# Block differences on GpSimd instead of VectorE, and a longer run of idle products at the start

## The chip, the cores and the metric

One core of a Trainium2 chip runs the kernel. Its engines work side by side, each through its own queue in order: TensorE (PE, with the weight loads shown apart as PEld), VectorE (DVE), ScalarE (ACT), GpSimd (POOL), and SyncE (SP), which issues most of the DMAs. The metric is device time in microseconds, the median of several executions. One more execution was taken with the hardware profiler, and every row shown below is from it.

## The reference

An encoder block for 1024 positions of width 1024, with 16 learned meta tokens ahead of them. Everything is float32.

```python
u = _rms_norm(h, pre_w)
z = u @ w_in                                  # one projection, split into q, k, v, gates
rq, rk, rv, rg, aq, ak, av, ag, gr, ga = _split_in(z)
...
o_r = _bidirectional_retention(rq, rk, rv, lg_f, lg_b)[:, META_PAD:]
...                                           # group norm per head
o_r = o_r * ret_nw * jax.nn.silu(rg)
y_r = o_r @ w_rb
...
o_a = _windowed_sink_attention(aq, ak, av, sink)
o_a = o_a * jax.nn.silu(ag)
y_a = o_a @ w_ab
mix = jax.nn.sigmoid(gr) * y_r + jax.nn.sigmoid(ga) * y_a
out = mix @ w_o
return h + _rms_norm(out, post_w)
```

## The kernel before

**Products in two halves.** A float32 matrix is kept as a high part of type `fp32r` and the rest, the low part. `mm3` (lines 74 to 79) forms a product from three matmuls: high by high on line 76, low by high on line 77, high by low on line 78. So whatever becomes an operand is split first: ScalarE or GpSimd copies the high part (`nc.scalar.copy`, or `pool_hi` on line 89), and VectorE takes the source minus the high part (`dve_lo`, line 92, two inputs in SBUF).

**The beginning.** While the first inputs are still on their way, TensorE runs products of a zeroed tile, `idle` (lines 310 to 313). Then come eight steps `qk0_mm(k)`, each over 128 rows of the width. For each step ScalarE makes the high part of x (line 333, tile `big`) and VectorE the low part (line 335).

**The early stages.** Retention by heads, then attention, up to about 545 us. There GpSimd makes high parts (line 89), adds rotary halves (line 195), scales attention weights (line 1442) and issues DMAs. Some of VectorE's block differences stand there too (`pre_sums`, line 802, tile `we`).

**The late phases.** From about 545 us on, the four large projections run as phases z (gates), r, a and o. Each multiplies 1024 by 1024 blocks, which are cut 2 by 2 and combined by a scheme with seven products in place of eight. `PROD` on line 931 names the seven, with left operands such as A11 or S1 (made of weight blocks) and right operands B11, B21, B22, T1, T2, T3 and T4. T1 to T4 are sums and differences of the blocks of the right matrix. `Phase.prepare` loads and splits a left operand (lines 976, 977; tiles `lhz`, `llz` in phase z, `lhr`, `llr` in r, `lha`, `lla` in a), six products ahead of its use (`LEAD = 6`). `Phase.product` issues a product: twelve matmuls of 512 columns into a PSUM bank (`bz`, `br`, `ba`). `combine` and the `post` functions take it out with VectorE and ScalarE: line 1066 adds a bank to a tile, line 1241 scales by `rbc`, line 1254 applies a gate, line 1280 a merge gate; line 1063 is a copy by ScalarE.

**The right operands.** Those of r, a and o change from phase to phase, and they are rebuilt while the phase before is still multiplying. `refill` loads four blocks of four 128-row slices from DRAM, takes the differences with `minus` (line 1155) and splits each result with `split_b` (line 952 by ScalarE, line 92 by VectorE; tiles `big` and `T`). With `nm == "z"` it prepares phase r and with `nm == "r"` phase a: in each of the two, `t1`, `t2`, `t3` and `b21` call `minus` four times. For phase o nothing is left to be subtracted at that time: `pre_split` (line 771) makes the differences of `w_out` during phase z, four for each of four slices (line 776, tile `w`), and stores their parts in DRAM, from where `get_pre` loads them. Their place is fixed by hooks: `hooks[12 * k + 22]` runs `pre_split(k, near[0])`, and `tc.issue_after(behind)` queues an instruction behind one named instruction, if both are on the same engine.

**The order.** The order in each engine's queue is made when the program is built, by a planner that runs through the program with estimated durations, within the dependencies and the `issue_after` marks. Engines and lines that are not edited can so stand in another order once something else is edited. Tiles are handed on by semaphores: an instruction waits for those that write what it reads, or that still read what it overwrites.

In the rows, `x` or a number behind a tile name is left out, so `llr<-wrr,lhr` is a low part of phase r made of a raw weight tile and its high part.

Of the kernel before, what the change touches and what calls it, by code (L numbers as in the profile page):

```python
# [10 lines left out]
ALU = mybir.AluOpType  # L11
# [23 lines left out]
def cols(c):  # L35
    return (0, NM) if c == 0 else (NM + P * (c - 1), NM + P * c)
# [3 lines left out]
def block_kernel(ctx: ExitStack, tc: tile.TileContext, x0, xT, x, meta, w_in, w_rb, w_ab, w_out, post_w,  # L40
                 rope, tab, out):
    nc = tc.nc
# [48 lines left out]
    def dve_lo(o, i, hi):  # L91
        return nc.vector.tensor_tensor(o, i, hi.bitcast(F32), ALU.subtract).ins  # L92
# [173 lines left out]
    with tc.tile_pool(name="setup", bufs=1, reuse_waits="tile") as st:  # L266
# [42 lines left out]

        idle = pj("idle")  # L310
        zeros = xm.rearrange("p k e -> p (k e)")
        for i in range(8):
            nc.tensor.matmul(idle[:, 0:KT * (32 + NM)], zeros[:, 0:P], zeros, start=True, stop=True)


# [44 lines left out]
        for c in range(9):  # L360
            a, b = cols(c)
# [409 lines left out]
    def pre_split(k, behind):  # L771

        x = w.pop(k)
        for n, o, a, b in SUMS:
            with tc.issue_after(behind):
                nc.vector.tensor_tensor(x[o], x[a], x[b], ALU.subtract)
            h, l = (stage(f"w{n}{k}{e_}", s, R) for s, e_ in enumerate("hl"))
            nc.scalar.copy(h, x[o])
            nc.sync.dma_start(pre_d[n][0][:, k], h.bitcast(F32))
            dve_lo(l, x[o], h)  # L780
            nc.sync.dma_start(pre_d[n][1][:, k], l.bitcast(F32))
# [160 lines left out]
    sub, mul, add = ALU.subtract, ALU.mult, ALU.add  # L942

    def stage(name, j=0, dt=F32):
        return (yp if j else lp).tile([P, 512], dt, tag=f"sg{int(j)}", bufs=8 if j else 7, name=name)
# [4 lines left out]
    def split_b(n, k, src):  # L950
        (h, as_), (l, _) = (right(n, s, k) for s in range(2))
        nc.scalar.copy(h, as_(src))
        dve_lo(l, as_(src), h)
# [174 lines left out]
    def get_pre(n):  # L1128
        for s in range(2):
            m = B[n][s].shape[1]  # L1130
            nc.sync.dma_start(B[n][s].bitcast(F32), pre_d[n][s][:, 0:m])
            if m < 4:
                d, as_ = right(n, s, m)
                nc.sync.dma_start(d.bitcast(F32), as_(pre_d[n][s][:, m]))
# [8 lines left out]
    def refill(nm, src):  # L1143

        x = {}

        def load(i, j):
            def f():
                for k in range(4):
                    x[i, j, k] = t = stage(f"{nm}{i}{j}{k}", j)  # L1150
                    src(t, 4 * i + k, j)
            return f

        def minus(o, a, b):
            nc.vector.tensor_tensor(x[*o], x[*a], x[*b], sub)

        def plain(n, i, j):
            def f():
                for k in range(4):
                    split_b(n, k, x[i, j, k])  # L1160
            return f

        def t1():
            for k in range(4):
                minus((0, 0, k), (0, 1, k), (0, 0, k))
                split_b("T1", k, x[0, 0, k])

        def t2():
            for k in range(4):
                minus((0, 0, k), (1, 1, k), (0, 0, k))  # L1170
                split_b("T2", k, x[0, 0, k])

        def t3():
            for k in range(4):
                minus((0, 1, k), (1, 1, k), (0, 1, k))

        def b21():
            for k in range(4):
                split_b("B21", k, x[1, 0, k])
                minus((0, 0, k), (1, 0, k), (0, 0, k))  # L1180

        def got(n):
            return lambda: get_pre(n)

        if nm == "a":
            return {-16: [load(0, 0)], -14: [load(1, 1)], -13: [plain("B11", 0, 0)], -11: [got("T1")],
                    -10: [load(1, 0)], -9: [got("T2")], -7: [plain("B21", 1, 0)], -5: [got("T3")],
                    -3: [plain("B22", 1, 1)], -1: [got("T4")]}
        return {-16: [load(0, 0), load(0, 1)], -14: [load(1, 1)], -13: [plain("B11", 0, 0)], -11: [t1],
                -10: [load(1, 0)], -9: [t2, t3], -7: [b21], -5: [plain("T3", 0, 1)], -3: [plain("B22", 1, 1)],  # L1190
                -1: [plain("T4", 0, 0)]}

    def run(phases):

        jobs = [(ph, u, p) for ph, _ in phases for u, p in ph.seq]
        hooks, i = {}, 0
        for ph, src in phases:
            i += len(ph.seq)
            if src:
                hooks.update({i + j: f for j, f in refill(ph.nm, src).items()})  # L1200

        for u in (0, 1):
            hooks.setdefault(len(jobs) - len(ph_o.seq) - 11 + u, []).insert(0, lambda u=u: ph_o.block(u, "A11"))
        for k in range(4):
            hooks[12 * k + 16] = [lambda k=k: pre_load(k, act_src(w_out))]
            hooks[12 * k + 22] = [lambda k=k: pre_split(k, near[0])]
        n = 0
        for i, (ph, u, p) in enumerate(jobs):
            while n < min(i + LEAD, len(jobs)):
                q, u_, p_ = jobs[n]  # L1210
                q.prepare(u_, p_)
                n += 1
            yield
            ph.product(u, p)
            for f in hooks.get(i, ()):
                f()
# [362 lines left out]
    i = attention()  # L1579
# [105 lines left out]
```

## Time and profile before

| what | value |
|---|---|
| median of 3 runs | 1043.71 us (1042.65 to 1046.04) |
| the profiled execution's own time | 1044.06 us |
| its span, first to last instruction | 1042.3 us |
| outside the span | 1.76 us |
| mean granted TensorE clock | 0.998 |
| busy: PE, DVE, ACT, POOL | 1025.3, 834.9, 502.5, 227.9 us |
| late phases, 550 us to the end (492.3 us): PE, DVE, ACT, POOL | 480.2, 421.1, 245.7, 26.8 us |

The page gives busy time by engine, then the span in 40 slices, then queues, chains and the costliest groups of instructions. A row of a group has its line, engine, operation and tiles. A timeline row begins with the start and the duration in microseconds; in square brackets stands how long the engine was idle before it, and what ended that. A row of the windows view has the stretch, its length, and for each engine the busy time with its number of instructions. Records of neighbouring instructions on one engine overlap a little, so the distance from start to start is what an instruction costs its engine.

### The profile page before, as it was taken

The numbers are of one execution on the slowest core, as the hardware profiler recorded it, in microseconds if no ns is written. First come the engines' busy times: TensorE is split into PE (matmuls) and PEld (weight loads), VectorE is DVE, ScalarE is ACT, GpSimd is POOL, SyncE is SP. The second block draws the span as 40 slices with busy tenths as digits, with TensorE's granted clock in tenths as the row PEclk, the third lists the DMA queues.
The fourth block names the chain that finished last, engine by engine and source line by source line (L and its number), as shares of the span: only waits on it lengthen the run. The fifth ranks groups of instructions, "written<-read, shape, count | busy, mean of one in ns | idle before, by whom it ended". The sixth has DMA issues, their size and how long they took to land. (4 is left out here: it accounts for less than half of the span.)

```text
span 1042.3 us, 17315 instructions
## 1 busy us (share of the span) xinstructions
PE 1025.3 (98%) x5880; PEld 898.8 (86%) x5880; DVE 834.9 (80%) x1802; ACT 502.5 (48%) x1129; POOL 227.9 (22%) x368
## 2 busy tenths in 40 slices
PE   8999999999999999999999999999999999999997
PEld 8998999989989888988888888777888788788886
DVE  7786769758876778778769988998899899778665
ACT  5541332523423466664676554555557446334443
POOL 3345244243342433444310000000000000111032
PEclk9999999999999999999999999999999999999999
DMA  9434123243241467675558679899925746789464
GB/s 355 164 84 90 62 45 89 76 79 112 80 93 62 102 174 188 179 194 157 171 174 322 216 255 311 309 317 346 392 106 178 251 156 222 234 219 336 130 122 81
DMA packets 98841, 188.45 MB, mean 181 GB/s; under 512 B 13025, under 2 KB 37633, under 8 KB 98193
## 3 DMA queue, kind: packets, MB, share of 16 engines
q1 hardware_dynamic: 81200, 162.89, 46.4%
q0 software_dynamic: 10176, 14.73, 9.5%
q10 hardware_dynamic: 7376, 9.73, 2.7%
q8 instruction: 46, 0.75, 0.3%
q14 instruction: 43, 0.34, 0.1%
HBM read 124.32 MB, written 57.68 MB: 175 GB/s over the span
## 5 line engine op out<-in xcount | busy, mean ns | idle before, releaser
L1289 POOL DMA_DIRECT2D mx_d<-c1a x4 | 3.6, 890 | 398.1 <-DVE c1a L1280 398.1
L77 PE MATMUL bz<-big,llz 128*128 128x512 f32 x192 | 74.8, 390 | 0.3 <-DVE llz L92 0.3
L76 PE MATMUL bz<-big,lhz 128*128 128x512 f32 x192 | 74.0, 390 | 1.1 <-ACT lhz L976 1.1
L78 PE MATMUL bz<-big,lhz 128*128 128x512 f32 x192 | 74.2, 389 | 0.0
L76 PE MATMUL pv<-wh,big 128*128 128x256 f32 x256 | 72.8, 284 | 0.0
L77 PE MATMUL pv<-wh,big 128*128 128x256 f32 x256 | 72.7, 284 | 0.0
L78 PE MATMUL pv<-wl,big 128*128 128x256 f32 x256 | 72.7, 284 | 0.0
L76 PE MATMUL bz<-T,lhz 128*128 128x512 f32 x176 | 68.2, 390 | 1.4 <-DVE u2z L1066 1.3
L77 PE MATMUL bz<-T,llz 128*128 128x512 f32 x176 | 68.6, 390 | 0.9 <-DVE llz L92 0.9
L78 PE MATMUL bz<-T,lhz 128*128 128x512 f32 x176 | 68.5, 389 | 0.0
L76 PE MATMUL paq<-big,wh 128*128 128x512 f32 x128 | 51.5, 403 | 0.0
L1429 ACT ACTIVATE p<-raw,nm 128x337 f32<-128x337 f32 (+1 forms) x64 | 35.5, 556 | 33.1 <-DVE nm L1426 31.6
L77 PE MATMUL paq<-big,wl 128*128 128x512 f32 x128 | 50.3, 393 | 0.0
L78 PE MATMUL paq<-big,wh 128*128 128x512 f32 x128 | 50.2, 392 | 0.0
L1442 POOL TENSOR_SCALAR p<-p,den 128x336 f32<-128x336 f32 (+2 forms) x60 | 34.6, 624 | 66.7 <-DVE den L1433 64.1
L76 PEld LDWEIGHTS pv<-wh,big 128*128 128x128 f32 x256 | 48.4, 189 | 0.4
L77 PEld LDWEIGHTS pv<-wh,big 128*128 128x128 f32 x256 | 48.3, 189 | 0.4
L78 PEld LDWEIGHTS pv<-wl,big 128*128 128x128 f32 x256 | 48.2, 188 | 0.3
L76 PEld LDWEIGHTS bz<-big,lhz 128*128 128x128 f32 x192 | 36.0, 188 | 8.8 <-ACT lhz L976 1.5
L92 DVE TENSOR_TENSOR wl<-wr,wh 128x1024 fp32r<-128x1024 f32 x28 | 35.1, 1257 | 10.0 <-POOL wh L89 6.8
L77 PEld LDWEIGHTS bz<-big,llz 128*128 128x128 f32 x192 | 36.0, 188 | 8.1 <-DVE llz L92 0.6
L78 PEld LDWEIGHTS bz<-big,lhz 128*128 128x128 f32 x192 | 36.0, 188 | 7.5
(621 smaller groups left out, 3592.8 us busy)
## 6 DMA issues: line engine op xcount, KB each, us to landing
wrz<-in_w_in_dram SPq DMA_DIRECT2D x32, 512.0 KB, 6.1
wr<-in_w_in_dram SPq DMA_DIRECT2D x29, 512.0 KB, 4.1
we<-in_w_in_dram SPq DMA_DIRECT2D x16, 512.0 KB, 4.3
tg<-tg_d SPq DMA_DIRECT2D x32, 256.0 KB, 4.9
e<-e ACTq DMA_DIRECT2D x20, 256.0 KB, 2.6
e<-e SPq DMA_DIRECT2D x20, 256.0 KB, 4.7
xn<-in_x_dram SPq DMA_DIRECT2D x8, 512.0 KB, 9.0
oTr_d<-ost SPq DMA_DIRECT2D x16, 256.0 KB, 2.1
```

The source lines that it names most:

```text
L76: nc.tensor.matmul(o, ah, bh, start=first, stop=False, **kw)
L77: nc.tensor.matmul(o, al, bh, start=False, stop=False, **kw)
L78: latest[:] = [nc.tensor.matmul(o, ah, bl, start=False, stop=last, **kw).ins]
L92: return nc.vector.tensor_tensor(o, i, hi.bitcast(F32), ALU.subtract).ins
L1289: nc.gpsimd.dma_start(d, to, accum_op=ALU.add)
L1429: last["exp"] = nc.scalar.activation(pp[:, x_, w0 - o:w0 - o + 1 + wid], r[:, 0:1 + wid], AF.Exp, scale=-1.0, bias=nm_[:, x_:x_ + 1], accu ...
L1442: nc.gpsimd.tensor_scalar(v, v, den[:, x_:x_ + 1], 1.0, op0=ALU.mult, op1=ALU.mult)
```

## The change

Two lines of code change their engine, `nc.vector` to `nc.gpsimd`: the differences in `pre_split` and those in `minus`. In all 48 instructions of 128 by 512 elements move from VectorE to GpSimd: 16 of line 776 and 32 of line 1155. The `issue_after(behind)` in `pre_split` names a VectorE instruction, while the instructions in it are now GpSimd's. In the beginning the loop of idle products runs 11 times instead of 8. The differences in `sum_row` (line 757), in `pre_sums` (line 802) and those of the left operands in `prepare` stay on VectorE.

```diff
-        for i in range(8):
+        for i in range(11):
             nc.tensor.matmul(idle[:, 0:KT * (32 + NM)], zeros[:, 0:P], zeros, start=True, stop=True)
...
         for n, o, a, b in SUMS:
             with tc.issue_after(behind):
-                nc.vector.tensor_tensor(x[o], x[a], x[b], ALU.subtract)
+                nc.gpsimd.tensor_tensor(x[o], x[a], x[b], ALU.subtract)
...
         def minus(o, a, b):
-            nc.vector.tensor_tensor(x[*o], x[*a], x[*b], sub)
+            nc.gpsimd.tensor_tensor(x[*o], x[*a], x[*b], sub)
```

## The prediction

> **What bounds the kernel now.** I read the page first, then the busy times by stretch, then TensorE's waits in the late phases, and last the timeline around those waits.
>
> ```profile
> span 1042.3 us, 17315 instructions
> PE 1025.3 (98%) x5880; PEld 898.8 (86%) x5880; DVE 834.9 (80%) x1802; ACT 502.5 (48%) x1129; POOL 227.9 (22%) x368
> DVE  7786769758876778778769988998899899778665
> POOL 3345244243342433444310000000000000111032
> PEclk9999999999999999999999999999999999999999
> ```
>
> TensorE is busy for 98% of the span, so the time can fall by little, but each pause of TensorE is time lost. From slice 22 to 33 VectorE is nearly full while GpSimd does nothing: there the change moves work. The stretches of the two refills, with all engines, then the part of VectorE's work that names a PSUM bank of the running phase (`bz` in the first, `br` in the second), then the moved lines:
>
> ```profile
> core 0: us, PE busy (x) PEld busy (x) DVE busy (x) ACT busy (x) POOL busy (x), PEclk, DMA share, GB/s
> 765.00:805.00 40.00, 40.00 (x178) 33.10 (x178) 39.97 (x67) 27.32 (x50) 0.00 (x0) 1.00 0.38 126
> 845.00:893.00 48.00, 47.11 (x208) 38.69 (x207) 47.01 (x79) 27.30 (x49) 0.00 (x0) 1.00 0.56 194
> ...
> 765.00:805.00 40.00, 37.31 (x164) 30.47 (x164) 5.33 (x8) 3.49 (x6) 1.00 0.38 126
> 845.00:893.00 48.00, 36.81 (x161) 29.76 (x159) 5.36 (x8) 3.50 (x6) 1.00 0.56 194
> ...
> L776 DVE TENSOR_TENSOR w<-w,w x16: 679/681/685, 616.8 to 721.0; 128x512 f32<-128x512 f32 x16
> L1155 DVE TENSOR_TENSOR z<-z,z x16: 678/682/685, 770.1 to 800.8; 128x512 f32<-128x512 f32 x16
> L1155 DVE TENSOR_TENSOR r<-r,r x16: 680/683/684, 849.0 to 877.8; 128x512 f32<-128x512 f32 x16
> ```
>
> In both refills VectorE has no time left: 39.97 of 40 us and 47.01 of 48. Per instruction that is 39.97/67 = 0.60 us. Of 67 instructions 16 are moved, 51 stay, and only 8 of these read PSUM; of 79, 63 stay and 8 read PSUM. TensorE's waits after 550 us, and the two places where a refill ends:
>
> ```profile
> PE bz L76 <- DVE u2z L1066: 1.3, 1, 1.3
> PE bz L76 <- ACT lhz L976: 1.1, 1, 1.1
> PE bz L77 <- DVE llz L92: 0.9, 1, 0.9
> PE ba L77 <- DVE lla L92: 0.9, 1, 0.9
> PE br L77 <- DVE llr L92: 0.8, 2, 0.6
> ...
> 811.63 0.67 DVE L92 TENSOR_TENSOR llr<-str1S,lhr 128x512 fp32r<-128x512 f32 x1
> 812.37 0.50 PE L77 MATMUL br<-big,llr 128*128 128x512 f32 x1 [0.23 <-DVE llr L92]
> 889.87 0.68 DVE L92 TENSOR_TENSOR lla<-sta1S,lha 128x512 fp32r<-128x512 f32 x1
> 890.61 0.50 PE L77 MATMUL ba<-big,lla 128*128 128x512 f32 x1 [0.89 <-DVE lla L92]
> ```
>
> The waits sum to 5.0 us. At 812.37 and 890.61 TensorE starts 0.07 and 0.06 us after VectorE's low part is done. The backlog of each refill has used up the lead of six products by then, so whatever VectorE loses or gains in a refill, TensorE loses at these places, or gains until its waits are gone.
>
> **Part 1: what a moved difference costs.** VectorE gets rid of 0.60 us for each. What it costs there depends on whether GpSimd's work holds VectorE up. The trace has the same operation on GpSimd, and VectorE's two-input instructions beside GpSimd:
>
> ```profile
> L195 POOL TENSOR_TENSOR kr<-m_qk,m_qk x4: 735/742/772, 30.9 to 43.8; 128x256 f32<-128x256 f32 x3, 128x272 f32<-128x272 f32 x1
> L195 POOL TENSOR_TENSOR qr<-m_qk,m_qk x2: 1285/1288/1292, 34.4 to 47.2; 128x512 f32<-128x512 f32 x2
> ...
> 43.81 0.74 POOL L195 TENSOR_TENSOR kr<-m_qk,m_qk 128x256 f32<-128x256 f32 x1 [1.49 <-DVE m_qk L194]
> 44.10 0.53 DVE L879 TENSOR_TENSOR qd<-rcol,dtab 128x64 f32<-128x64 f32 x1
> 40.02 0.20 DVE L384 TENSOR_TENSOR kdr<-r,dtab 128x64 f32<-128x64 f32 x1
> ...
> 241.85 0.61 POOL L89 TENSOR_SCALAR qh<-qr 128x512 fp32r<-128x512 f32 x1
> 241.93 0.81 DVE L92 TENSOR_TENSOR Slb<-Sb,Shb 128x256 fp32r<-128x256 f32 x1
> 91.12 0.41 DVE L92 TENSOR_TENSOR Slb<-Sb,Shb 128x256 fp32r<-128x256 f32 x1
> ```
>
> From 256 to 512 columns GpSimd's subtraction grows from 742 to 1288 ns: 2.13 ns a column, so 1.09 us of its 1.29 is in the data and 0.20 is fixed. VectorE's `qd` starts while GpSimd adds, and it ends 0.08 us after GpSimd's end (44.63 against 44.55), in 0.53 us where its like takes 0.20. `Slb` takes 0.81 us beside GpSimd's copy and 0.41 without it: 0.40 us more, where the copy of 0.61 has some 0.41 in its data (0.61 less the fixed 0.20). So a VectorE instruction with two SBUF inputs waits out GpSimd's data time. I take 1.10 us of wait for each moved difference, met by the share of VectorE's work that has no PSUM input: 43/51 = 0.84 in the first refill, 55/63 = 0.87 in the second. Below, it is bounded by nothing (GpSimd meets only gaps and PSUM readers), above by GpSimd's whole 1.29. I take 1.10, since `qd` and `Slb` show nearly that.
>
> [...]
>
> First refill: 51 × 0.60 = 30.6 us of work and 16 × 1.10 × 0.84 = 14.8 of waits, 45.4 for 40.0 before: +5.4. Second: 63 × 0.60 = 37.8 and 16 × 1.10 × 0.87 = 15.3, 53.1 for 48: +5.1. Both show on TensorE at the two places above.
>
> For `pre_split` the same price gives 4 × (1.10 × 0.85 − 0.60) = +1.3 us for each of its four slices, at 617 to 721 us. The first has no wait of TensorE behind it. Behind the other three stand the waits for `lhz`, `u2z` and `llz` (1.1, 1.3 and 0.9 us). But VectorE waits here too:
>
> ```profile
> 710.74 0.69 DVE L1002 TENSOR_TENSOR stz10S<-wrz,wrz 128x512 f32<-128x512 f32 x1 [3.17 <-DMA wrz<-in_w_in_dram]
> ```
>
> So part of the loss falls into time that is idle anyway. The bounds are −3.3 us (the three waits gone, nothing lost) and 4 × 1.3 = +5.2; I take half of three slices, +2.0. GpSimd has no instruction of its own between 550 and 900 us (the zeros of its row on the page), so no queued DMA stands behind a difference; behind each stand only ScalarE's copy and VectorE's low part of that slice. The DMAs of `pre_split` are SyncE's before and after.
>
> **Part 2: the idle products.**
>
> ```profile
> 1.36 2.93 PE L313 MATMUL idle<-xm 128*128 128x384 f32 x8 [1.36 <-DVE warm L207]
> 5.53 0.77 PE L76 MATMUL pq<-big,w 128*128 128x512 f32 x1 [1.24 <-ACT big L333]
> 7.83 0.63 PE L77 MATMUL pq<-big,w 128*128 128x512 f32 x1
> 9.98 0.59 PE L78 MATMUL pq<-big,w 128*128 128x512 f32 x1
> 10.65 0.39 PE L76 MATMUL pq<-big,w 128*128 128x512 f32 x1
> 7.49 1.16 ACT L333 ACTIVATE big<-xr,vec 128x1040 fp32r<-128x1040 f32 x1 [1.47 <-DVE w L92]
> ```
>
> The same 512 columns take 0.63 us until about 9.98 and 0.39 from 10.65 on: TensorE gets its full pace 4.45 us after its work became unbroken at 5.53 (the granted clock, PEclk, is 9 in all slices and doesn't show this). Eight idle products last 2.93 us and leave 1.24 us empty. Three more at some 0.34 us end at 1.36 + 2.93 + 1.02 = 5.31, so the first real product isn't pushed back, and the gap falls to 0.22 us. If that no longer breaks the stretch, the full pace comes 4.45 us after 1.36, at 5.81; what takes until 10.65 would end at 5.81 + (10.65 − 5.81)/2 = 8.2, and the second slice of x is ready on ScalarE at 7.49 + 1.16 = 8.65. TensorE then starts it at 8.65 in place of 10.65: a gain of 2.0 us, which stays as TensorE hardly waits behind it. Below it is bounded by 0 (0.22 us still breaks it). I take 2.0, as 0.22 is nearer to no gap than to 1.24.
>
> [...]
>
> **The sum.** 5.4 + 5.1 + 2.0 − 2.0 = +10.5 us against the profiled execution's own 1044.06 us (span 1042.3), which is 0.35 over the median 1043.71: 1054.6, told as 1054.5.
>
> **The rivals.** *VectorE is relieved (faster).* The planner may spread the differences to where VectorE reads PSUM or waits. They cost VectorE nothing from a share of 0.60/1.10 = 0.55 downward; near zero, all five waits (5.0 us) go too: 1044.06 − 5.0 − 2.0 = 1037, and with half of that 1040. For it: GpSimd is free, and a difference could be done ahead of its turn. Against: 84 to 87% of the neighbours have two SBUF inputs, and `t1`, `t2` and `t3` issue four differences in a row. Chance 0.15.
>
> *It cancels.* The share comes out near 0.6 and the waits stay: 1044.06 + 2 − 2 = 1044. Chance 0.13.
>
> *GpSimd's results are late.* VectorE's queue is in order, and a low part planned for a faster GpSimd holds up everything behind it. If a difference takes 1.10 + 0.60 us in alternation with VectorE, four in a row take 6.8 us, where four on VectorE take 2.4. Two such delays of 4.4 us on top of the sum, one for each refill, give 1063. Against: six products of lead, some 16 us at 12 × 0.225 us each (TensorE's 40.00/178). Chance 0.12.
>
> A measurement of this kernel can tell about 0.3%, 3.1 us, from no change: below 1040.6 is faster, over 1046.8 slower. My forecast has 0.60; its own range, by bounds of the wait and of `pre_split`, is 1047 to 1061. Together: faster 0.15, within 0.3% 0.13, slower 0.72. The range from 1039 to 1062 leaves out the far ends of the first and the last rival.
>
> **What would show it.** Right: L1155 and L776 on GpSimd at 1.3 us and often more; VectorE's L92 in the refills no longer 0.68 throughout but many at 1.2 to 1.8; TensorE's waits for `llr` and `lla` after the refills up from 0.8 and 0.9 us to some 5 each; the 0.39 us products from about 6 us on. Wrong: L92 at 0.68 beside GpSimd's differences, and waits for low parts gone, which is the first rival; VectorE idle ahead of `big` and `T` low parts until ScalarE or GpSimd, which is the last; the first refill's end moved by less than 2 us, which would undo the price of 1.10.

## The result, and the profile after

The changed kernel took 1071.36 us (median of 5 runs, 1069.04 to 1074.31) against 1043.46 us for the kernel before in the same comparison (5 runs, 1042.65 to 1046.04). The ratio is 1.0269 (95% interval 1.0244 to 1.0293): 27.9 us slower. The prediction was 1054.5, at most 1062: the sign was right and the size was far off. The profiled execution of the changed kernel took 1074.31 us, 30.25 more than that of before (1044.06).

The head of the page after:

```profile
span 1072.5 us, 17382 instructions
PE 1035.3 (97%) x5883; PEld 904.4 (84%) x5883; DVE 853.1 (80%) x1754; ACT 502.9 (47%) x1129; POOL 309.8 (29%) x416
POOL 3344243242432334343202340000072054010042
PEclk9999999999999999999999899999998998999999
```

VectorE has 48 instructions less (1754 for 1802) and is busy 18.2 us longer (853.1 for 834.9). TensorE's clock has three slices that are not 9. The zeros of GpSimd's row are now filled in two refills, and in slices 21 to 23 (counted from 0) as well, which is 563 to 643 us: earlier than the 616.8 to 721.0 us at which line 776 stood before. The groups of the moved lines say so exactly:

```profile
L776 POOL TENSOR_TENSOR w<-w,w x16: 1275/1622/3697, 568.7 to 641.4; 128x512 f32<-128x512 f32 x16
L1155 POOL TENSOR_TENSOR z<-z,z x16: 1269/1733/1747, 781.8 to 815.3; 128x512 f32<-128x512 f32 x16
L1155 POOL TENSOR_TENSOR r<-r,r x16: 1267/1737/1747, 870.2 to 901.6; 128x512 f32<-128x512 f32 x16
```

VectorE in the first refill, from the timeline (start, duration):

```profile
787.96 1.78 DVE L92 TENSOR_TENSOR llz<-wrz,lhz 128x512 fp32r<-128x512 f32 x1
789.66 1.78 DVE L92 TENSOR_TENSOR llz<-stz14S,lhz 128x512 fp32r<-128x512 f32 x1
791.36 1.78 DVE L92 TENSOR_TENSOR big<-z,big 128x512 fp32r<-128x512 f32 x1
793.06 1.77 DVE L998 TENSOR_TENSOR stz15S<-wrz 128x512 f32<-128x512 f32 x1
...
807.84 0.68 DVE L1066 TENSOR_TENSOR c1z<-c1z,bz 128x512 f32<-128x512 f32 x1
808.43 1.37 DVE L92 TENSOR_TENSOR T<-z,T 128x512 fp32r<-128x512 f32 x1
809.73 0.68 DVE L92 TENSOR_TENSOR llz<-wrz,lhz 128x512 fp32r<-128x512 f32 x1
```

From start to start it is 1.70 us, VectorE's own 0.60 and 1.10 of waiting, about once for each of GpSimd's differences. The instruction that reads the PSUM bank `bz` costs its 0.6 us (807.84 to 808.43), and so does a low part when GpSimd has nothing to do (809.73). So the price of 1.10 us, on which the prediction rested, is what the chip shows.

TensorE's waits after 545 us, and then four stretches with all engines (length; busy time and number of instructions of PE, PEld, DVE, ACT, POOL; granted clock, DMA share, GB/s):

```profile
PE bz L76 <- ACT u3z L1063: 6.4, 1, 6.4
PE bz L76 <- ACT u2z L1063: 4.2, 5, 2.0
PE br L76 <- DVE u3r L1066: 4.1, 1, 4.1
PE bz L76 <- ACT lhz L976: 3.0, 2, 2.1
PE bz L77 <- DVE llz L92: 3.0, 2, 2.2
PE br L77 <- DVE llr L92: 2.6, 1, 2.6
```

```profile
784.00:810.00 26.00, 22.28 (x99) 18.11 (x97) 26.00 (x21) 12.28 (x22) 23.30 (x14) 0.97 0.09 31
870.00:891.00 21.00, 21.00 (x95) 17.38 (x93) 21.00 (x15) 11.76 (x22) 20.33 (x12) 1.00 0.08 26
813.00:818.00 5.00, 5.00 (x12) 3.87 (x13) 4.96 (x8) 3.00 (x7) 1.28 (x1) 0.50 0.93 318
819.00:824.00 5.00, 5.00 (x24) 4.11 (x23) 5.00 (x9) 2.90 (x6) 0.00 (x0) 1.00 0.90 255
```

In 26 us of the first refill VectorE gets 21 instructions done, where 0.60 us each would make 43. The longest wait is no longer one for a low part: at 806 us TensorE stands 6.4 us because its PSUM bank isn't free. ScalarE's copy (line 1063) empties it, and ScalarE had stood 5.5 us at an instruction ahead of that copy, until VectorE had done line 1241:

```profile
811.05 0.63 ACT L1245 ACTIVATE c1z<-c1z 128x512 f32<-128x512 f32 x1 [5.52 <-DVE c1z L1241]
811.59 0.60 ACT L976 CAST lhz<-wrz 128x512 fp32r<-128x512 f32 x1
812.10 0.58 ACT L1063 COPY u3z<-bz 128x512 f32<-128x512 f32 x1
```

So VectorE's backlog reaches TensorE through ScalarE's queue here. Behind that wait comes a loss that the prediction had no term for: from 813 to 818 us TensorE is busy without a pause and does 12 matmuls, at a granted clock of 0.50; six us later it does 24 in the same time.

### The profile page after: what moved, and what is told of

Same layout as the page of the kernel before. It is cut to its first block, busy times and chain, and to the rows that moved or that the text cites. A ratio compares the mean times of both kernels' runs of the same rounds, so it can differ in the third digit from the quotient of the medians.

```text
span 1072.5 us, 17382 instructions
## 1 busy us (share of the span) xinstructions
PE 1035.3 (97%) x5883; PEld 904.4 (84%) x5883; DVE 853.1 (80%) x1754; ACT 502.9 (47%) x1129; POOL 309.8 (29%) x416
## 5 line engine op out<-in xcount | busy, mean ns | idle before, releaser
L76 PE MATMUL bz<-T,lhz 128*128 128x512 f32 x176 | 71.6, 408 | 15.3 <-ACT u3z L1063 6.4
L77 PE MATMUL bz<-T,llz 128*128 128x512 f32 x176 | 70.8, 402 | 2.2 <-DVE llz L92 2.2
L78 PE MATMUL bz<-T,lhz 128*128 128x512 f32 x176 | 70.4, 400 | 0.0
L1155 POOL TENSOR_TENSOR z<-z,z 128x512 f32<-128x512 f32 x16 | 26.2, 1667 | 147.3 <-DVE big L92 139.4
L76 PEld LDWEIGHTS bz<-T,lhz 128*128 128x128 f32 x176 | 34.2, 195 | 25.9 <-ACT u3z L1063 6.9
L776 POOL TENSOR_TENSOR w<-w,w 128x512 f32<-128x512 f32 x16 | 28.3, 1767 | 84.8 <-DMA w<-in_w_out_dram 44.7
L187 POOL DMA_DIRECT2D aq<-m_aq x32 | 27.5, 979 | 63.3 <-DVE aq L185 34.7
```

Of the source, the lines that this page charges most:

```text
L76: nc.tensor.matmul(o, ah, bh, start=first, stop=False, **kw)
L77: nc.tensor.matmul(o, al, bh, start=False, stop=False, **kw)
L78: latest[:] = [nc.tensor.matmul(o, ah, bl, start=False, stop=last, **kw).ins]
L187: nc.gpsimd.dma_start(o[64 - r:128 - r, 0:n], m[r:r + 64, 0:n], accum_op=ALU.add)
L776: nc.gpsimd.tensor_tensor(x[o], x[a], x[b], ALU.subtract)
L1155: nc.gpsimd.tensor_tensor(x[*o], x[*a], x[*b], sub)
```

## The experiments

Every time is a median beside runs of the kernel before on the same chip, whose medians were 1042.04 (17 runs; the first four kernels), 1042.34 (13; the next four), 1042.05 (13; the two with a cut `pre_split`) and 1042.12 (7; the last three). Each edit also lets the planner put some other instructions in another order; that is part of every number here.

**The idle products alone.**

```diff
-        for i in range(8):
+        for i in range(11):
```

> Only the loop of idle products is changed, 8 to 11. The profile after shows TensorE's full pace from about 6 us on and the second slice of x begun 2 us earlier. Theory (the gap of 0.22 us no longer breaks the stretch): the time falls by 2.0 us, to some 1041.5. Rival (the 2 us are lost again at a wait of TensorE further on, or come in some executions alone): no change, 1043.5, or executions scattered between.

Measured: 1041.61 us, ratio 0.999 (0.9981 to 0.9998): 0.4 us gained by the medians, about 1 us by the ratio. No other kernel of this study has a median below that of the kernel before, and this one is hardly further below it than the measurement can tell. TensorE's beginning in it, and then in a kernel of a later experiment (`pre_split` with the cut and its own mark) that has eight idle products, as before:

```profile
1.36 3.67 PE L313 MATMUL idle<-xm 128*128 128x384 f32 x11 [1.36 <-DVE warm L207]
5.49 0.47 PE L76 MATMUL pq<-big,w 128*128 128x512 f32 x1 [0.46 <-ACT big L333]
5.79 0.39 PE L77 MATMUL pq<-big,w 128*128 128x512 f32 x1
...
9.04 0.47 PE L76 MATMUL pq<-big,w 128*128 128x512 f32 x1 [0.49 <-ACT big L333]
```

```profile
1.36 2.93 PE L314 MATMUL idle<-xm 128*128 128x384 f32 x8 [1.36 <-DVE warm L208]
5.55 0.48 PE L76 MATMUL pq<-big,w 128*128 128x512 f32 x1 [1.26 <-ACT big L334]
5.87 0.39 PE L77 MATMUL pq<-big,w 128*128 128x512 f32 x1
...
8.52 0.47 PE L76 MATMUL pq<-big,w 128*128 128x512 f32 x1
```

With eleven idle products the full pace is there at the second real product, about as forecast (5.81). But the second kernel has a gap of 1.26 us, as long as before, and the full pace comes just as early. So it isn't shown that the gap of 1.24 us held the pace back in the trace before; the moment of the full pace differs from one execution to the next (10.65 us in the trace before, 5.87 in the second kernel). In the traces of the eleven kernels with eight idle products the second slice starts at 8.52 to 10.65 us, 10.08 in the mean; in the four with eleven products at 8.60 to 9.10, 8.96 in the mean. The trace before, from which the 2.0 us were worked out, is the latest of all. The means differ by 1.1 us, which agrees with the 1 us of the ratio.

**Each of the two moves alone.** First only line 776, then only line 1155:

```diff
-                nc.vector.tensor_tensor(x[o], x[a], x[b], ALU.subtract)
+                nc.gpsimd.tensor_tensor(x[o], x[a], x[b], ALU.subtract)
```

> Only the 16 differences of pre_split go to GpSimd. In the profile after, TensorE's waits and half-pace products between 545 and 690 us come to 18.2 us, against 5.2 before, and these differences ran at 569 to 643 us instead of 617 to 721. If the two moves are independent, this kernel loses 13 us: some 1056.5. Rival (the loss came from the planner's order under both moves together): within 4 us of 1043.5.

```diff
-            nc.vector.tensor_tensor(x[*o], x[*a], x[*b], sub)
+            nc.gpsimd.tensor_tensor(x[*o], x[*a], x[*b], sub)
```

> Only the 32 differences of the two refills go to GpSimd. In the profile after, TensorE's losses at 800 to 820 us and 890 to 910 us are 9.6 and 10.1 us, against 1.3 and 1.5 before. If the moves are independent: +16.9 us, some 1060.5, with VectorE's two-input instructions 1.70 us apart (0.60 of their own and 1.10 of GpSimd's) as long as GpSimd's differences run back to back. Rival (prediction's size, 1.10 us times a share of 0.85 and no more): +10.5, some 1054.

Measured: `pre_split` 1057.40 us, ratio 1.0142 (1.0125 to 1.0158), 15.4 us; the refills 1060.08 us, 1.0167 (1.0150 to 1.0184), 18.0 us. With the idle products that makes some 33 us against the 27.9 of the whole change, so the moves together cost some 5 us less than the sum of each by itself. Sixteen differences in `pre_split` cost almost as much as thirty-two in the refills, and the prediction had given them 2.0 of 12.5.

**The place without the engine.** In `pre_split` the differences stay on VectorE and only the mark goes, which is what the change does to it by the way: the marked instruction is VectorE's and can't hold one of GpSimd's back.

```diff
-            with tc.issue_after(behind):
-                nc.vector.tensor_tensor(x[o], x[a], x[b], ALU.subtract)
+            nc.vector.tensor_tensor(x[o], x[a], x[b], ALU.subtract)
```

> The 16 differences of pre_split stay on VectorE, but the mark that queues them behind a named VectorE instruction is taken away, as it stops binding when they are GpSimd's. Theory (place: the differences come some 50 us earlier and with them their loads and stores, into the stretch in which phase z starts): a large part of the loss of e2, 6 us or more, over 1049.5. Rival (port: the loss of e2 is GpSimd's hold on VectorE's second input): less than 3 us, under 1046.5, since nothing runs on GpSimd.

Measured: 1051.72 us, ratio 1.0091 (1.0075 to 1.0107), 9.7 us with no instruction on GpSimd. The stretches of this kernel, then the same of before:

```profile
560.00:600.00 40.00, 38.60 (x171) 31.64 (x169) 39.97 (x67) 24.83 (x44) 0.00 (x0) 1.00 0.84 282
600.00:650.00 50.00, 46.66 (x204) 38.33 (x205) 46.06 (x77) 26.33 (x47) 0.00 (x0) 1.00 0.98 345
```

```profile
560.00:600.00 40.00, 40.00 (x178) 33.11 (x178) 38.66 (x65) 22.77 (x41) 0.00 (x0) 1.00 0.70 238
600.00:650.00 50.00, 50.00 (x222) 41.44 (x221) 42.30 (x71) 24.61 (x44) 0.00 (x0) 1.00 0.85 284
```

From 560 to 600 us VectorE had 1.3 us of idle time left; with the differences there it has none, and TensorE begins to wait. The DMA share rises as well, from 0.70 to 0.84 and from 0.85 to 0.98; which of the two costs more wasn't taken apart.

**GpSimd's reads by themselves.** All differences stay on VectorE. Beside each of the 32 in the refills GpSimd does something that nobody needs, into a tile that nothing reads: two subtractions of 256 columns, or four constants of 256 columns (and a subtraction of one column, which keeps them in place).

```diff
-        def minus(o, a, b):
+        def minus(o, a, b, after=None):
             nc.vector.tensor_tensor(x[*o], x[*a], x[*b], sub)
+            c = x[*a] if after is None else right(after, 1, o[2])[0].bitcast(F32)
+            t = gp.tile([P, 256], F32, tag="scr", bufs=1, name=f"scr{nm}{o}")
+            for r in (0, 256):
+                nc.gpsimd.tensor_tensor(t, x[*a][:, r:r + 256], c[:, r:r + 256], sub)
```

> The kernel before, with all differences on VectorE; beside each of the 32 differences of the refills GpSimd runs two useless subtractions of 256 columns into a tile of its own that nothing reads. No result of GpSimd is waited for, and VectorE keeps all its work. Theory (VectorE waits out GpSimd's reads): each useless pair holds VectorE up to 1.10 us, 16 to 17 us in each refill with none of the 0.60 us relief; the loss is larger than the 18 us of the refills' differences on GpSimd, 1062 to 1078 in all. Rival (the loss of the change comes from results of GpSimd that come late in VectorE's queue): no change, 1042 within 3 us.

```diff
...
+            nc.gpsimd.tensor_tensor(t[:, 0:1], x[*a][:, 0:1], c[:, 0:1], sub)
+            for r in range(4):
+                nc.gpsimd.memset(t, float(r))
```

> As the kernel with the useless subtractions, but GpSimd sets its own tile to a constant four times instead, 256 columns each, so that it writes and reads almost nothing (one subtraction of one column keeps the place). Theory (what holds VectorE up is GpSimd reading two inputs beside VectorE's two): 1042 to 1046. Rival (any work of GpSimd, its writes too, holds VectorE up for its data time): 1055 or more.

Measured: useless subtractions 1070.76 us, ratio 1.0273 (1.0252 to 1.0294); constants 1042.57 us, ratio 1.0000 (0.9989 to 1.0010). VectorE's line 1155 in the first kernel, and in the second, where a row of GpSimd's constants stands with it:

```profile
L1155 DVE TENSOR_TENSOR z<-z,z x16: 675/1215/1233, 768.0 to 813.0; 128x512 f32<-128x512 f32 x16
```

```profile
L1155 DVE TENSOR_TENSOR z<-z,z x16: 681/684/692, 768.0 to 798.9; 128x512 f32<-128x512 f32 x16
L1160 POOL MEMSET scrz(0, 0, 0)_9901<- x4: 312/314/315, 767.6 to 768.7; 128x256 f32 x4
```

Nobody waits for these results, so the 28 us can't come from late results. They come from GpSimd's reads, as the constants, which only write, cost nothing (ratio 1.0000): a subtraction of 256 columns makes a VectorE instruction last 1.22 us for 0.68, that is 0.54 more, and 256 columns at the 2.13 ns of the prediction are 0.55.

**The old place, with GpSimd.** GpSimd's differences are put back behind the marked instruction through a one-column copy. In the first form the copy reads the tile that this instruction wrote; with `pre_split` alone (shown here against the kernel before), then in the whole change:

```diff
+    place = mhalf[:, 39:40]
...
+        mark = pool_hi(place, behind[:, 0:1])
...
-            with tc.issue_after(behind):
-                nc.vector.tensor_tensor(x[o], x[a], x[b], ALU.subtract)
+            with tc.issue_after(mark):
+                nc.gpsimd.tensor_tensor(x[o], x[a], x[b], ALU.subtract)
...
-                near[:] = [nc.vector.tensor_tensor(o, i, st[at][0], add).ins]
+                near[:] = [nc.vector.tensor_tensor(o, i, st[at][0], add).ins, o]
...
-            hooks[12 * k + 22] = [lambda k=k: pre_split(k, near[0])]
+            hooks[12 * k + 22] = [lambda k=k: pre_split(k, near[1])]
```

> Only the sixteen differences of pre_split are on GpSimd, and they keep their place: a copy of one column by GpSimd reads the tile that the marked VectorE instruction wrote, and the differences are queued behind that copy. The earlier place alone cost 9.5 us with the differences on VectorE (1051.7 against 1042.0), and place and engine together 14.8 (1057.4). Theory (place and port add up): 1042 + 14.8 - 9.5 = 1047, range 1044 to 1050, differences from about 617 to 722 us. Rival (GpSimd's differences cost this much wherever they stand): 1057 as without the place, over 1053 in any case.

> The whole change, with pre_split's differences on GpSimd kept in the place that they had before, by the same copy of one column. Theory (the lost place is a term of its own of 9 to 10 us): 1071.4 - 9.5 = 1062, range 1058 to 1065. Rival (the place doesn't matter once the refills are slow, since the delays overlap): over 1067.

Measured: `pre_split` alone 1052.53 us, ratio 1.0097 (1.0077 to 1.0117), 10.2 us where 5 were expected; the whole change 1064.48 us, ratio 1.0219 (1.0195 to 1.0242). The first miss spoke for late results, as ScalarE stood 4.3 us at one first high copy. So `pre_split` was cut in two: the differences two products earlier, the high copies and low parts later, once on GpSimd and once on VectorE (the diff shows the second; the first has the one-column copy as its mark).

```diff
-            hooks[12 * k + 22] = [lambda k=k: pre_split(k, near[0])]
+            hooks[12 * k + 20] = [lambda k=k: pre_diff(k, near[0])]
+            hooks.setdefault(12 * k + 28, []).insert(0, lambda k=k: pre_split(k))
...
+            with tc.issue_after(later[0]):
+                nc.scalar.copy(h, x[o])
```

> pre_split is cut in two: the four differences run on GpSimd two products earlier than before, behind a copy of one column as their mark, and the high copies on ScalarE and the low parts on VectorE are queued four instructions in a row behind a later copy of ScalarE. So the differences have about 5 us and more of slack before ScalarE needs them. Without the slack they cost 10.2 us (1052.5), and ScalarE's queue stood up to 4.3 us at the first copy. Theory (half or more of the 10.2 us comes from ScalarE's queue standing behind a late difference): 1044 to 1048, and no wait of ScalarE for a difference of over 1 us. Rival (it is VectorE's lost time alone, 1.1 us for each difference against 0.6 saved, and its knock-on): 1050 or more, ScalarE's waits gone or not.

> The same cut of pre_split in two, with the differences left on VectorE: what the cut and the shift by two products cost or bring by themselves. Theory: within 3 us of 1042, so that the comparison of the two kernels with the cut tells the cost of the engine alone. Rival (every shift of these instructions from their hand-made place costs, as the loss of the mark did with 9.5 us): 1047 or more.

Measured: on GpSimd 1057.03 us, ratio 1.0143 (1.0123 to 1.0163); on VectorE 1044.27 us, 1.0020 (1.0008 to 1.0031). No ScalarE instruction waits for a difference any more, and the differences still cost 12.8 us more on GpSimd than on VectorE: ScalarE's wait for them was not the cause. One wait in the first of the two, in VectorE's queue, came from the mark itself:

```profile
DVE u3z L1263 <- POOL mhalf L89: 4.0, 1, 4.0
```

VectorE rewrites the tile that the copy reads. So the mark was moved to a one-column VectorE instruction on a column of `mhalf` that nothing else uses, queued behind the same instruction (the diff is against the first form); with the cut, with the uncut `pre_split`, and in the whole change.

```diff
-        mark = pool_hi(place, behind[:, 0:1])
+        with tc.issue_after(behind):
+            nc.vector.tensor_tensor(mhalf[:, 38:39], mhalf[:, 0:1], mhalf[:, 0:1], ALU.add)
+        mark = pool_hi(place, mhalf[:, 38:39])
```

> As the kernel with pre_split cut in two and its differences on GpSimd, but the mark is a one-column VectorE instruction on a tile of its own, queued behind the same instruction as before, and GpSimd's one-column copy reads that. VectorE no longer has to wait for the copy before it rewrites a product's tile (4.0 us at once in the kernel before this one). Theory (the mark was part of the 12.8 us): 1046 to 1052, that is 2 to 8 us over the same cut with the differences on VectorE (1044.3). Rival (the engine costs over 10 us even with slack and a harmless mark): over 1054.

> pre_split whole, its differences on GpSimd at the old place, behind the harmless mark. Theory (place and engine are separate terms, 9.5 of the 14.8 us is place): 1044 to 1048, and the first differences within 1 us of 616.8 us. Rival (late differences hold ScalarE's and SyncE's queues up at the old place, where nothing has slack): 1050 or more, with ScalarE's waits for a difference of 2 us and more.

> The whole change, with pre_split's differences on GpSimd at the old place, behind the harmless mark. From the runs so far: 1071.4 less the cost of the lost place, 6.9 us by the first kind of mark (1064.5). Theory (the first mark cost something itself): 1058 to 1063. Rival (it cost nothing): 1064 or more.

Measured: with the cut 1055.67 us, ratio 1.0130 (1.0103 to 1.0157); uncut at the old place 1050.67 us, 1.0083 (1.0054 to 1.0111), 8.5 us; the whole change 1066.50 us, 1.0233 (1.0214 to 1.0252). In the second of these the mark stands where the first difference stood before (616.80 us), and GpSimd and VectorE go on so:

```profile
616.63 0.68 DVE L92 TENSOR_TENSOR llz<-stz5S,lhz 128x512 fp32r<-128x512 f32 x1
616.80 2.98 POOL L89 TENSOR_SCALAR mhalf<-mhalf 128x1 f32<-128x1 f32 x1 [87.16 <-DVE mhalf L776]
...
619.04 0.68 DVE L1008 TENSOR_TENSOR stz5S<-stz5S,wrz 128x512 f32<-128x512 f32 x1
619.64 0.68 DVE L1070 TENSOR_TENSOR u2z<-u2z,bz 128x512 f32<-128x512 f32 x1
619.74 6.41 POOL L780 TENSOR_TENSOR w<-w,w 128x512 f32<-128x512 f32 x4
620.24 1.33 DVE L92 TENSOR_TENSOR llz<-stz4S,lhz 128x512 fp32r<-128x512 f32 x1
621.06 0.62 ACT L782 CAST wT10h<-w 128x512 fp32r<-128x512 f32 x1 [2.43 <-POOL w L780]
621.71 1.57 DVE L92 TENSOR_TENSOR wT10l<-w,wT10h 128x512 fp32r<-128x512 f32 x1
```

GpSimd's copy of one column lasts 2.98 us, until VectorE, after five instructions with two SBUF inputs, comes to one that reads PSUM (`bz`, 619.64). Then the four differences take 6.41 us and VectorE waits its turn. ScalarE stands 2.43 us for the first. So at the old place, too, four differences of 0.60 us each become, with the copy ahead of them, a step of 9.4 us here and of 7.4 to 8.1 us in the other three slices.

What follows for `pre_split`: the engine at the undisturbed place costs 8.5 us, and the lost place 6.7 more (1057.40 against 1050.67), or 4.9 in the whole change (1071.36 against 1066.50). These depend on each other: the place alone was 9.7 with the differences on VectorE. The expectations of these three kernels were missed on the same side, each time for its rival: the first mark's cost was not what kept `pre_split` dear. In the second of them the differences still began 2.9 us late (619.74), held up by the copy ahead of them, so the engine's 8.5 us holds that too.

One thing stays open. With the cut and the harmless mark it is 11.4 us more on GpSimd than on VectorE. VectorE waits there for raw weights, in this stretch and the one behind it:

```profile
DVE stz12S L1012 <- DMA wrz<-in_w_in_dram: 4.4, 1, 4.4
DVE stz8S L1012 <- DMA wrz<-in_w_in_dram: 2.8, 1, 2.8
```

With the differences on VectorE such waits are 1.2 us at the most. Why those loads come later wasn't isolated.

## Why the prediction was wrong in size, step by step

TensorE's loss can be taken from the trace. A matmul of 512 columns starts 0.227 us behind the last one at full pace. What the steps around a wait have beyond this is the wait; steps of 0.37 to 0.46 us without one are half pace. Summed, in us, as waits and half pace:

| kernel | 545 to 745 us | 745 to 845 | 845 to 930 |
|---|---|---|---|
| before | 5.1 + 0 | 1.3 + 0 | 1.3 + 0.2 |
| after | 15.1 + 2.9 | 7.0 + 2.6 | 7.9 + 2.2 |
| `pre_split` alone | 14.7 + 2.8 | 0.7 + 0 | 1.3 + 0.2 |
| refills alone | 3.6 + 0 | 7.0 + 1.2 | 6.4 + 2.8 |
| `pre_split` on VectorE, no mark | 11.0 + 1.4 | 0.7 + 0 | 1.3 + 0.2 |
| `pre_split` on GpSimd, old place, harmless mark | 11.4 + 0 | 1.4 + 0 | 1.3 + 0.2 |
| useless subtractions | 2.8 + 0 | 13.0 + 2.6 | 12.0 + 4.2 |

*The price, 1.10 us: right.* VectorE's steps beyond 0.601 us beside GpSimd's differences sum to 16.0 us in each refill of the changed kernel. That is 1.00 for each of 16, a share of 0.91 where 0.84 and 0.87 were taken. The prediction's upper bound was GpSimd's whole 1.29 us; the steps of 1.70 us say 1.10. That VectorE's work with a PSUM input has no part in it was the author's estimate; the step of 0.59 us from 807.84, beside a difference that GpSimd began at 807.99, agrees with it.

*First and second refill, +5.4 and +5.1: right as waits.* They measured 7.0 − 1.3 = 5.7 and 7.9 − 1.3 = 6.6; with the refills alone 5.7 and 5.1. VectorE's own balance, 16.0 − 16 × 0.60 = 6.4 in each, is the same size. But the place was another: not the low parts `llr` and `lla` after the refills, but PSUM banks that came free late within them (6.4 and 4.1 us), and one low part, `llr`, in the second (2.6 us).

*`pre_split`, +2.0, at most +5.2: the step that failed.* It was priced at 617 to 721 us, with half of three slices, because VectorE sometimes waits there. Two things are wrong in that. The differences didn't stay there: the diff leaves the mark without effect, the planner put them at 569 to 641 us, and VectorE was full (38.66 of 40 us). The text ahead of the prediction said that a mark binds only on one engine, and the prediction made no step of it. And at the old place the halving was wrong: VectorE loses 15.1 us beside the sixteen, saves 9.6, and these 5.5 show in full and more on TensorE, as 11.4 − 5.1 = 6.3 us of waits and 8.5 us of time. VectorE's waits come in four blocks of 3.4 to 4.0 us, where GpSimd's differences stand in a row; its idle time elsewhere doesn't cover them. Measured in the whole change: waits of 15.1 − 5.1 = 10.0 us.

*No term at all: half pace.* 2.9 + 2.6 + 2.2 − 0.2 = 7.5 us. It stands behind long waits: between 545 and 930 us, in the traces of before and of all fourteen changed kernels, every stretch of four and more matmuls at half pace has a wait of 1.9 us or more in the 7 us ahead of it. The prediction had waits of 5 us in its own sum, and in its part on the beginning it had TensorE go slowly behind a gap; it gave the pace behind a wait no term.

*The start, −2.0:* −1.6 between these two traces (the second slice at 9.10 us for 10.65), about −1.1 in the mean of all. The forecast was worked out from one execution, in which the full pace came late. A gain between its two bounds, 0 and 2.0 us, fits better.

Together: 5.7 + 6.6 + 10.0 + 7.5 − 1.6 = 28.2 of the 30.25 us between the two profiled executions. The rest isn't assigned. The rival of relief is refuted by the steps of 1.70 us. Late results, with 6.8 us for four differences in alternation, named a size that is right (6.4 us, four in a row), but in the refills it isn't needed: the useless subtractions, whose results are never late for anyone, cost 28 us.

## What to carry to other kernels

In these runs GpSimd's work was free for VectorE where it only wrote SBUF (the constants: ratio 1.0000), or stood beside a VectorE instruction that takes an input from PSUM (0.60 us a step). Beside VectorE instructions with two SBUF inputs, count the data time of each moved instruction against the time that VectorE saves (here 1.10 against 0.60 us). When an instruction changes its engine, look for every mark and order that names its old engine, and cost the step at the place where it will then stand. A sum that makes TensorE wait for several microseconds at once needs a further term for the pace behind each wait (7.5 us here).

## What the runs showed of the hardware that was not expected

*GpSimd was held up as well.* A GpSimd instruction that reads one column lasted 2.98 us beside a dense run of VectorE, and 5.66 us in the kernel with the constants, where VectorE's steps of 0.60 us went on beside it:

```profile
770.94 5.66 POOL L1158 TENSOR_TENSOR scrz(0, 0, 2)_9919<-z,big 128x1 f32<-128x1 f32 x1
771.05 0.69 DVE L1155 TENSOR_TENSOR z<-z,z 128x512 f32<-128x512 f32 x1
771.65 0.69 DVE L92 TENSOR_TENSOR big<-z,big 128x512 fp32r<-128x512 f32 x1
```

The first ended when VectorE came to an instruction that reads PSUM, the second at 776.60 us in a pause of 0.1 us between two VectorE instructions; whether that pause let it in or was its doing, the trace doesn't tell. So a read of one column by GpSimd took 2.98 and 5.66 us beside VectorE's two-input instructions, where others like them took 0.56 us (the copy in the last slice of the first kernel) and 0.24 us (at 769.14 us in the second). In the refills of the changed kernel, where GpSimd's differences stand in a row, the two alternate one by one (1.70 us a step).

*Half pace comes behind a long wait, but not behind one of a fixed length.* A wait is counted here as in the table, from start to start less 0.227 us. In the fifteen traces all eight waits of TensorE of 3.36 us and more, between 545 and 930 us, were followed by a stretch of 2.5 to 5.6 us at half pace. Between 2.0 and 3.1 us it varied: waits of 2.54 and 2.66 us were followed by one, and waits of 2.93, 3.01 and 3.08 us weren't. So the length of the wait alone doesn't settle it, and what does stays open.
